# A decoder layer on one core: the input projection's last eight K tiles in two passes for six column blocks, and the modulation's VectorE share as row sums over a transposed copy

## The chip, the core and the metric

One NeuronCore of a Trainium2 chip runs the whole program, with TensorE (PE), VectorE (DVE), ScalarE (ACT), GpSimd (POOL) and SyncE (SP, which here only issues DMAs). The metric is the device time in microseconds (us) of one execution; the time of a kernel is the median of its runs.

## What is computed

A decoder layer for 256 tokens, width 2048, fp32, cut to what matters here:

```python
mod = silu(c) @ w_ada + b_ada                       # w_ada: 2048 x 12288, one vector c
shift_a, scale_a, gate_a, shift_f, scale_f, gate_f = split(mod, 6)
h = rms_norm(x, g_attn_pre) * (1 + scale_a) + shift_a
proj = h @ w_in                                     # 2048 x 5456
# columns: diff q | k | v (1024 each), dsa q (1024) | k | v (128 each), indexer q (1024) | k | w
diff_out = rms_norm((softmax(q1 k1) - lam * softmax(q2 k2)) v)      # 8 heads, causal
score = sum_h w_h * relu(iq_h . ik)                 # 16 indexer heads; the 64 best keys of a query
dsa_out = softmax(q k over those keys) v            # 8 heads
x = x + gate_a * rms_norm([diff_out, dsa_out] @ w_o)
h = rms_norm(x, g_ffn_pre) * (1 + scale_f) + shift_f
x = x + gate_f * rms_norm((silu(h @ w_gate) * (h @ w_up)) @ w_down)
```

## The kernel before

**Weights.** `wload` brings 1 MB of a weight matrix (mostly 4 K tiles of 128 rows by 512 columns) into one of five `raw` buffers. ACT rounds it to `whi` (line 168), DVE subtracts to get the rest `wlo` (line 169), in two halves of 128x1024; there are three buffers of each. A product of a K tile with a token tile is three matmuls (`mm3`, lines 178, 181, 182): 24 matmuls for a megabyte. All these loads stand in the one queue of SP, in the order in which the program issues them.

**Modulation.** The product of silu(c) with `w_ada` is cut into 96 units of 1 MB. `ada_block` makes a unit on PE (line 225: four matmuls, which the trace records as eight) or on DVE (line 233: four `scalar_tensor_tensor` that add a column block times one element of silu(c) to the accumulator `aacc`). 64 units go to PE and 32 to DVE: two of four blocks of the attention gate `Ga`, one of four of `modF` (shift and scale ahead of the FFN), and all of the FFN's gate `Gf`. `ada_step` uses the next unit and keeps two units of loads ahead.

**Projection.** The K tiles are taken in groups of 1, 1, 2, 4 and 8 (`GROUPS`), each a pass over the 11 blocks of 512 columns; after the first pass DVE adds each bank to `PR` (line 733). During a pass the modulation of the next group's rows is made. The last pass, K tiles 8 to 15, goes through the blocks in the order 0, 2, 4, 10, 9, 8, 1, 3, 5, 6, 7. As a block becomes complete, `attend` rotates it and queues jobs: heads of the differential attention (`diff_head`), the indexer's scores (`idx_pairs`, line 422), `top_k` (lines 454 and 455), and the indexed heads (`dsa_pair`). `attn_step` moves every job in flight by one stage, once after each megabyte.

**Output projection and after.** `mixT` holds the attention's output, transposed; K tiles 0 to 7 are the differential heads, 8 to 15 the indexed ones. The first two column blocks of w_o take the rest of the attention along; the other two are made by `tail_pair`, after which `residual` runs for each token tile: the block times the gate into `y` (line 768), the square sum `sst`, its root `rs`, the new `x` (line 843), then the diagonal `dg` (line 848) with which PE makes the transposed `h2` (line 830). The first FFN blocks use only K tiles 0 to 7 of `h2`, while the rest of `modF` is made. Then gate, up and down projections in three groups.

**Order.** The program is scheduled at build time: every engine gets a fixed order of instructions, and an engine waits where its next one is not ready.

## Time and profile before

| | |
|---|---|
| runs | 1273.87, 1273.33, 1276.59 us, median 1273.87 |
| profiled execution, span from first to last instruction | 1272.5 us |
| PE busy | 1233.9 us (97%) |
| DVE busy | 774.3 us (61%) |
| ACT busy | 560.9 us (44%) |
| HBM read | 307.05 MB, 243 GB/s over the span |

The profiled execution's span is 1.4 us under the median time of the runs. Shares of busy time are means over stages that differ: the stages' own bounds are read from tables by window.

### The profile page before, as it was taken

Reading aid. Unit: us, or ns where it says so; the run is one execution under the profiler, and the core shown is the slowest. Engines: PE = TensorE matmul, PEld = TensorE weight load, DVE = VectorE, ACT = ScalarE, POOL = GpSimd, SP = SyncE. Lnnn points to the kernel's source line nnn. Section 1 sums busy time; section 2 is a strip of 40 time slices with the busy share of each in tenths; the row PEclk is TensorE's granted clock in tenths of the full one; section 3 lists DMA queues with packets and bytes.
Section 4 is the critical chain, followed back from the end, with each engine's and each line's share of the span. In section 5 each row is a group of like instructions: output and inputs, shape, how many; then the busy total and the mean of one; then the engine's idle time right before and its main releaser. Section 6 shows DMA issues by size and latency. Waiting matters only on the chain.

```text
span 1272.5 us, 15272 instructions
## 1 busy us (share of the span) xinstructions
PE 1233.9 (97%) x5938; PEld 950.3 (75%) x5938; DVE 774.3 (61%) x1160; ACT 560.9 (44%) x806; POOL 21.4 (2%) x55
## 2 busy tenths in 40 slices
PE   4999999999999999899999999999999999999996
PEld 3666666777666786688887888888888888888885
DVE  3576455898598683758867545754455454445565
ACT  4733333345345543764444444444444334444442
POOL 1000000000000000200000000000000000000000
PEclk8999999999999999999999999999999999999998
DMA  9999997978687487858878656766556555565541
GB/s 307 339 343 327 347 381 278 314 263 321 211 285 268 142 329 289 306 167 286 282 264 290 200 193 222 251 227 198 176 189 199 190 188 190 194 198 182 184 164 66
DMA packets 160090, 310.13 MB, mean 244 GB/s; under 512 B 5785, under 2 KB 19978, under 8 KB 158738
## 3 DMA queue, kind: packets, MB, share of 16 engines
q1 hardware_dynamic: 159938, 309.14, 70.7%
q8 instruction: 46, 0.75, 0.2%
q14 instruction: 26, 0.21, 0.0%
q10 hardware_dynamic: 80, 0.02, 0.0%
HBM read 307.05 MB, written 2.10 MB: 243 GB/s over the span
## 4 chain that ended last, share of the span: by engine, by line
PE 88%; DMA 4%; DVE 4%; issue 1%; ACT 1%; SPq 1%; POOL 0%; DVEq 0%; POOLq 0%; ACTq 0%
PE mm L181 26%; PE mm L178 26%; PE mm L182 25%; PE ad L225 5%; DMA raw<-in_w_ada_dram 4%; DVE aacc L233 2%; DVE wlo L169 1%; PE tr L474 1%; PE tr L411 1%; PE tr L918 1%; PE tr L830 1%; SPq L211 1%; PE tr L392 1%; PE tr L301 0%; PE tr L282 0%
## 5 line engine op out<-in xcount | busy, mean ns | idle before, releaser
L169 DVE TENSOR_TENSOR wlo<-raw,whi 128x1024 fp32r<-128x1024 f32 (+1 forms) x383 | 462.3, 1212 | 338.6 <-ACT whi L168 337.7
L168 ACT ACTIVATE whi<-raw 128x1024 fp32r<-128x1024 f32 (+1 forms) x383 | 400.3, 1050 | 522.4 <-PE mm L182 458.1
L181 PE MATMUL mm<-wlo,h 128*128 128x512 f32 (+1 forms) x1056 | 416.8, 395 | 1.9 <-DVE wlo L169 1.9
L182 PE MATMUL mm<-whi,h 128*128 128x512 f32 (+1 forms) x1056 | 409.9, 389 | 0.2 <-DVE h L335 0.2
L178 PE MATMUL mm<-whi,h 128*128 128x512 f32 (+1 forms) x1056 | 381.4, 394 | 2.4 <-ACT h L330 1.4
L181 PEld LDWEIGHTS mm<-wlo,h 128*128 128x128 f32 x1056 | 198.9, 188 | 62.5 <-issue 9.5
L178 PEld LDWEIGHTS mm<-whi,h 128*128 128x128 f32 x1056 | 196.8, 188 | 63.2 <-issue 13.6
L182 PEld LDWEIGHTS mm<-whi,h 128*128 128x128 f32 x1056 | 198.3, 188 | 42.5 <-issue 3.0
L181 PE MATMUL mm<-wlo,gT 128*128 128x512 f32 x348 | 135.8, 390 | 0.0
L182 PE MATMUL mm<-whi,gT 128*128 128x512 f32 x348 | 135.4, 389 | 0.0
L178 PE MATMUL mm<-whi,gT 128*128 128x512 f32 x348 | 123.0, 390 | 0.0
L233 DVE SCALAR_TENSOR_TENSOR aacc<-raw,csil,aacc 128x512 f32<-128x512 f32 x126 | 94.1, 746 | 23.8 <-DMA raw<-in_w_ada_dram 22.5
L225 PE MATMUL ad<-raw,c 128*32 128x512 f32 (+2 forms) x640 | 79.6, 537 | 9.9 <-DMA raw<-in_w_ada_dram 9.9
L733 DVE TENSOR_TENSOR PR<-mm,PR 128x512 f32<-128x512 f32 (+1 forms) x88 | 57.1, 669 | 41.2 <-PE mm L182 41.0
L182 PEld LDWEIGHTS mm<-whi,gT 128*128 128x128 f32 x348 | 65.3, 188 | 13.8 <-issue 0.2
L181 PEld LDWEIGHTS mm<-wlo,gT 128*128 128x128 f32 x348 | 65.3, 188 | 13.7 <-issue 0.2
L178 PEld LDWEIGHTS mm<-whi,gT 128*128 128x128 f32 x348 | 65.3, 188 | 13.4
L181 PE MATMUL mm<-wlo,mixT 128*128 128x512 f32 x124 | 49.1, 397 | 0.0
L178 PE MATMUL mm<-whi,mixT 128*128 128x512 f32 x124 | 47.5, 400 | 0.6 <-ACT mixT L587 0.6
L182 PE MATMUL mm<-whi,mixT 128*128 128x512 f32 x124 | 46.4, 399 | 0.0
L225 PEld LDWEIGHTS ad<-raw,c 128*32 128x32 f32 x640 | 17.6, 116 | 36.4 <-issue 31.3
L181 PEld LDWEIGHTS mm<-wlo,mixT 128*128 128x128 f32 x124 | 23.3, 188 | 7.8 <-issue 2.5
(195 smaller groups left out, 678.8 us busy)
## 6 DMA issues: line engine op xcount, KB each, us to landing
raw<-in_w_ada_dram SPq DMA_DIRECT2D x96, 1024.0 KB, 7.1
raw<-in_w_gate_dram SPq DMA_DIRECT2D x44, 1024.0 KB, 5.2
raw<-in_w_up_dram SPq DMA_DIRECT2D x44, 1024.0 KB, 5.1
raw<-in_w_down_dram SPq DMA_DIRECT2D x44, 1024.0 KB, 5.2
raw<-in_w_in_dram SPq DMA_DIRECT2D x39, 1024.0 KB, 6.9
raw<-in_w_o_dram SPq DMA_DIRECT2D x16, 1024.0 KB, 5.0
xx<-in_x_dram SPq DMA_DIRECT2D x2, 1024.0 KB
x<-in_x_dram SPq DMA_DIRECT2D x2, 1024.0 KB, 4.7
```

The source lines that it names most:

```text
L168: ACT.activation(hv, src, AF.Copy)
L169: DVE.tensor_tensor(lv, src, hv.bitcast(F32), op=ALU.subtract)
L178: i = PE.matmul(ps, lhsT=hi, rhs=whi, start=start, stop=False)
L181: PE.matmul(ps, lhsT=hi, rhs=wlo, start=False, stop=False)
L182: PE.matmul(ps, lhsT=lo, rhs=whi, start=False, stop=stop)
L211: SP.dma_start(st[b, u], ada_w[u * kk * P:(u + 1) * kk * P, col0s[b]:col0s[b] + n] .rearrange("(k p) n -> p k n", p=P))
L225: PE.matmul(st["ps"][32 * j:32 * j + 32, :n], lhsT=c33[:, k, 1 - b:33 - b], rhs=w, start=(b == 0 and k < 4), stop=(b == nb - 1 and k >= 12 ...
L233: DVE.scalar_tensor_tensor(acc, w, csil[:, k:k + 1], acc, op0=ALU.mult, op1=ALU.add)
L392: PE.transpose(tr[:, i * P:(i + 1) * P], PR[:, t, c0:c0 + P], ident)
L411: PE.matmul(sc[i][:, SEG[t]], lhsT=st["q"][r, (2 * j + t) * P:(2 * j + t + 1) * P], rhs=ikT[r, :P * (t + 1)], start=True, stop=True)
L474: PE.matmul(sc[i][:, SEG[t]], lhsT=l, rhs=r, start=False, stop=(t == T - 1))
L733: DVE.tensor_tensor(dst, banks[c0][t][:, :n], dst, op=ALU.add)
```

## The change

The last group of eight K tiles becomes two groups of four. The six column blocks that come first (`EARLY`) get a pass over K tiles 8 to 11 and one over 12 to 15; the other five (`LATE`) get one pass over all eight, with one more `attn_step` inside each block. The attention's jobs and the loads of `Ga` start with the second of these passes; before that, only A, the modulation that the projection itself needs, is loaded. A unit on DVE is no longer a megabyte of rows of `w_ada`, but 128 rows of a transposed copy `w_adaT` that the host prepares: one `tensor_tensor_reduce` over 128x2048 multiplies it by `csrow` (silu(c) on every partition) and sums along the row, starting from the bias; the result is a column. `spread` turns a column into a row on all partitions: a DVE multiply with the identity, a matmul with ones, and for `csrow` a copy by ACT. On DVE are now the last 4 K tiles of A (8 units), two blocks of `Ga` (8), two of `modF` (16) and all of `Gf` (16): 48 units, and 48 on PE. The two halves of the big shared buffer (`bigB`) are now tiles of their own, `big0` and `big1`.

```diff
-GROUPS = (1, 1, 2, 4, 8)
+GROUPS = (1, 1, 2, 4, 4, 4)
+A_DVE = (5,)
-F_DVE = (2,)
-A_DVE = ()
+F_DVE = (1, 2)
-ATT = 1
+EARLY = (0, 2, 4, 10, 9, 8)
+LATE = (1, 3, 5, 6, 7)
...
+    def ada_rows(col0, dst, bias, finish=None):
...
+        def load():
+            st["raw"] = wp.tile([P, 2048], F32, tag="raw", name=nm("raw"), bufs=RAW)
+            SP.dma_start(st["raw"], w_adaT[col0:col0 + P])
+
+        def use():
+            DVE.tensor_tensor_reduce(out=st["raw"], in0=st["raw"], in1=csrow, scale=1.0, scalar=bias(),
+                                     op0=ALU.mult, op1=ALU.add, accum_out=dst())
+            if finish is not None:
+                after.append(finish)
+
+        units.append((load, use))
+
+    def spread(row, col):
...
+        m = wp.tile([P, 512], F32, tag="aacc", name=nm("dg"), bufs=2)
+        DVE.tensor_tensor(m.rearrange("p (k q) -> p k q", k=4),
+                          ident[:, None, :].to_broadcast([P, 4, P]),
+                          col[:, :, None].to_broadcast([P, 4, P]), op=ALU.mult)
+        ps = tr_bank()
+        PE.matmul(ps, lhsT=ones, rhs=m, start=True, stop=True)
+        if row is None:
+            return ps
+        ACT.activation(row, ps, AF.Copy)
...
+        for i in range(4):
+            ada_rows(c0 + i * P, lambda i=i: part(i),
+                     lambda i=i: bcol[:, col // P + i:col // P + i + 1],
+                     (lambda: DVE.tensor_tensor(g, spread(None, st["g"]), g, op=ALU.mult))
+                     if i == 3 else None)
...
+    passes = [(0, 1, every), (1, 1, every), (2, 2, every), (4, 4, every), (8, 4, EARLY),
+              (12, 4, EARLY), (8, 8, LATE)]
+    for pi, (k0, nk, blks) in enumerate(passes):
+        first, last = pi == 0, pi >= 5
+        if pi == 5:
+            mixT[0] = Halves("mixT", KT)
...
+                        mm3(banks[c0][t][:, :n], *Hs[k], t, whi, wlo, k == k0, k == k0 + nk - 1)
+                    if nk == 8 and k == k0 + 5:
+                        attn_step()
...
-        gT = big.tile([P, 2, 16, S], F32R, tag="bigB", name=nm("gT"))
+        gT = Halves("gT", 16)
```

What this does to the order is shown at three places. First, the queue of SP in the pass over K tiles 4 to 7 (`raw` from `in_w_in` is a weight load, from `in_w_ada` a unit of modulation). Before:

```order
L152 DMA raw_1049<-in_w_in_dram 128x4x512
L211 DMA raw_1091<-in_w_ada_dram 128x4x512
L211 DMA raw_1097<-in_w_ada_dram 128x4x512
L152 DMA raw_1099<-in_w_in_dram 128x4x512
L211 DMA raw_1141<-in_w_ada_dram 128x4x512
L211 DMA raw_1147<-in_w_ada_dram 128x4x512
```

Of the change:

```order
L163 DMA raw_1067<-in_w_in_dram 128x4x512
L220 DMA raw_1109<-in_w_ada_dram 128x4x512
L163 DMA raw_1111<-in_w_in_dram 128x4x512
L220 DMA raw_1153<-in_w_ada_dram 128x4x512
L163 DMA raw_1155<-in_w_in_dram 128x4x512
```

Two units of modulation stood behind each weight load; now one does. From the pass's first weight load to its last the queue held 16 units, and now holds 8.

Second, DVE around the top-k (MAX and MATCH_REPLACE on `nsel`; `mx`, `rcp`, `w`, `s`, `on` and the L641 write of `mixT` belong to the differential heads). Before, in the last blocks of the projection:

```order
L454 MAX m_2456<-nsel 128x8
L484 TENSOR_REDUCE mx_2911<-tr_2902 128x1 x2
L454 MAX m_2456<-nsel 128x8
L455 MATCH_REPLACE nsel<-m_2456,nsel 128x128
L484 TENSOR_REDUCE mx_2911<-tr_2903 128x1 x2
L485 TENSOR_SCALAR mx_2911<-mx_2911 128x2
L455 MATCH_REPLACE nsel<-m_2456,nsel 128x256
L169 TENSOR_TENSOR wlo_3242<-raw_3239,whi_3241 128x1024
L454 MAX m_2456<-nsel 128x8
L485 TENSOR_SCALAR mx_2911<-mx_2911 128x2
L169 TENSOR_TENSOR wlo_3246<-raw_3239,whi_3245 128x1024
```

Of the change, in the first half of the output projection, the last split before the top-k and the first one after it:

```order
L180 TENSOR_TENSOR wlo_3585<-raw_3582,whi_3584 128x1024
L475 SCALAR_TENSOR_TENSOR score<-rl_2611,iwS,score 128x128
L475 SCALAR_TENSOR_TENSOR score<-rl_2611,iwS,score 128x256
L475 SCALAR_TENSOR_TENSOR score<-rl_2650,iwS,score 128x128
L475 SCALAR_TENSOR_TENSOR score<-rl_2650,iwS,score 128x256
L258 ISA raw_3741,modF<-raw_3741,csrow,cols_244 128x2048
```

```order
L614 SCALAR_TENSOR_TENSOR s_3070<-s_3070,w_3145 128x256
L155 TENSOR_SCALAR rs_3138<-ss_3134 128x2
L633 TENSOR_SCALAR on_3133<-tr_3129,rcp_3050,rsd_3137 128x128 x2
L180 TENSOR_TENSOR wlo_3589<-raw_3582,whi_3588 128x1024
L180 TENSOR_TENSOR wlo_3651<-raw_3648,whi_3650 128x1024
```

The weight splits that stood among the rounds of the top-k are gone from there: 90 rows of DVE lie between the splits of the two halves of one `raw`, among them 14 of the 30 rows that add indexer scores (L475), the whole top-k, two of the row sums (L258) and most rows of four differential heads.

Third, DVE at the residual of token tile 0. Before:

```order
L768 TENSOR_TENSOR y<-mm_3920,Ga 128x512
L768 TENSOR_TENSOR y<-mm_3922,Ga 128x512
L839 TENSOR_REDUCE sst<-ssy 128x1
L144 TENSOR_SCALAR rs_4228<-sst 128x1
L843 SCALAR_TENSOR_TENSOR x_3897<-y,ry,x_3897 128x1024 x2
```

Of the change:

```order
L829 TENSOR_TENSOR y<-mm_3844,Ga 128x512
L258 ISA raw_4344,modF<-raw_4344,csrow,cols_244 128x2048
L258 ISA modF 128x1
L829 TENSOR_TENSOR y<-mm_3846,Ga 128x512
L899 TENSOR_REDUCE sst<-ssy 128x1
L258 ISA raw_4347,modF<-raw_4347,csrow,cols_244 128x2048
L258 ISA modF 128x1
L155 TENSOR_SCALAR rs_4122<-sst 128x1
```

Two row sums (each a row over 128x2048 and one that writes the 128x1 result) now stand between `y` and `rs`.

## Rows read from the trace of the kernel before

**Rows 1.** The page: busy time by engine, granted TensorE clock in 40 slices.
```profile
PE 1233.9 (97%) x5938; PEld 950.3 (75%) x5938; DVE 774.3 (61%) x1160; ACT 560.9 (44%) x806; POOL 21.4 (2%) x55
...
PEclk8999999999999999999999999999999999999998
```
**Rows 2.** The page: the chain of work that ended last, by engine.
```profile
PE 88%; DMA 4%; DVE 4%; issue 1%; ACT 1%; SPq 1%; POOL 0%; DVEq 0%; POOLq 0%; ACTq 0%
```
**Rows 3.** Windows by stage: us, busy time and instructions by engine, PEclk, DMA, GB/s.
```profile
112.80:194.50 81.70, 80.94 (x405) 52.25 (x402) 41.83 (x56) 29.62 (x40) 0.00 (x0) 1.00 0.98 358
194.50:283.20 88.70, 88.70 (x430) 61.48 (x429) 67.05 (x140) 35.34 (x66) 1.75 (x3) 1.00 0.80 277
283.20:375.70 92.50, 92.50 (x481) 60.41 (x480) 69.94 (x190) 38.79 (x74) 3.01 (x3) 1.00 0.76 269
375.70:459.00 83.30, 78.27 (x430) 60.31 (x429) 62.15 (x151) 44.67 (x119) 3.86 (x4) 1.00 0.65 228
459.00:518.40 59.40, 57.25 (x274) 40.85 (x272) 36.23 (x44) 24.16 (x35) 4.51 (x6) 1.00 0.84 302
518.40:572.90 54.50, 52.95 (x268) 42.46 (x267) 33.00 (x66) 37.91 (x74) 2.67 (x6) 1.00 0.69 242
708.90:1272.50 563.60, 553.26 (x2469) 457.75 (x2467) 294.89 (x284) 235.94 (x252) 1.11 (x2) 0.99 0.57 189
```
**Rows 4.** Waits from 112.8 to 194.5: us in total, times, longest.
```profile
DVE PR L733 <- PE mm L182: 28.3, 10, 5.3
ACT whi L168 <- DMA raw<-in_w_in_dram: 20.0, 4, 8.3
```
**Rows 5.** A window in the FFN, PE alone: us, busy (x matmuls).
```profile
720.00:795.00 75.00, 75.00 (x330) 1.00 0.62 202
```
**Rows 6.** The chain in order of time, one unit of modulation: start, us.
```profile
111.86 0.99 PE ad L225 x8
```
**Rows 7.** PE on tiles `tr` alone, output projection's first half: us, busy (x).
```profile
375.70:459.00 83.30, 32.50 (x213) 1.00 0.65 228
```
**Rows 8.** DVE groups by form: busy us, mean ns; idle before.
```profile
L169 DVE TENSOR_TENSOR wlo<-raw,whi 128x1024 fp32r<-128x1024 f32 x374 | 455.4, 1223 | 334.9 <-ACT whi L168 334.0
L233 DVE SCALAR_TENSOR_TENSOR aacc<-raw,csil,aacc 128x512 f32<-128x512 f32 x126 | 94.1, 746 | 23.8 <-DMA raw<-in_w_ada_dram 22.5
L733 DVE TENSOR_TENSOR PR<-mm,PR 128x512 f32<-128x512 f32 x80 | 53.5, 686 | 41.2 <-PE mm L182 41.0
...
L961 DVE SCALAR_TENSOR_TENSOR ff<-ff,ry,x 128x512 f32<-128x512 f32 x8 | 5.5, 744 | 0.7 <-POOL ry L145 0.7
...
L843 DVE SCALAR_TENSOR_TENSOR x<-y,ry,x 128x1024 f32<-128x1024 f32 x4 | 5.0, 1281 | 1.8 <-POOL ry L145 1.8
```
**Rows 9.** ACT groups by form: the read of a row sum from the accumulator.
```profile
L487 ACT ACTIVATION_READ_ACCUMULATOR s<-tr,mx 128x1 f32 x48 | 9.7, 203 | 0.0
```
**Rows 10.** DVE by time at the top-k: start, us.
```profile
356.67 0.61 DVE L454 MAX8 m<-score 128x8 f32<-128x128 f32 x2
...
363.43 1.21 DVE L169 TENSOR_TENSOR wlo<-raw,whi 128x1024 fp32r<-128x1024 f32 x1
...
364.82 1.22 DVE L169 TENSOR_TENSOR wlo<-raw,whi 128x1024 fp32r<-128x1024 f32 x1
```
**Rows 11.** All engines by time at the residual: start, us.
```profile
507.03 0.69 DVE L768 TENSOR_TENSOR y<-mm,Ga 128x512 f32<-128x512 f32 x1 [4.45 <-ACT tr L767]
...
508.64 2.48 DVE L843 SCALAR_TENSOR_TENSOR x<-y,ry,x 128x1024 f32<-128x1024 f32 x2 [0.66 <-POOL ry L145]
...
511.64 2.78 PE L225 MATMUL ad<-raw,c 128*32 128x512 f32 x24
...
515.90 0.61 POOL L848 TENSOR_SCALAR dg<-ident,r 128x128 f32<-128x128 f32 x1
```
**Rows 12.** DMA issues: count, KB each, median us from issue to landing.
```profile
raw<-in_w_ada_dram SPq DMA_DIRECT2D x96, 1024.0 KB, 7.1
...
x<-in_x_dram SPq DMA_DIRECT2D x2, 1024.0 KB, 4.7
```

More of the change, by code (lines that the diff above doesn't have):

```diff
@@ L276, in ada_cols, with finish @@
         m, k0 = n // P, col // P
-        def finish(accs):
+        d = dst[:, :, k0:k0 + m]
+        def finish(acc):
             ps = tr_bank()
             for i in range(m):
-                if len(accs) == 1:
-                    PE.matmul(ps[:, 2 * i:2 * i + 2], lhsT=accs[0][:, i * P:(i + 1) * P], rhs=sel,
-                              start=True, stop=True)
-                else:
-                    for b in range(2):
-                        PE.matmul(ps[:, 2 * i + b:2 * i + b + 1], lhsT=accs[b][:, i * P:(i + 1) * P],
-                                  rhs=ones[:, 0:1], start=True, stop=True)
-            d = dst[:, :, k0:k0 + m]
-            DVE.tensor_tensor(d, ps[:, :2 * m].rearrange("p (m b) -> p b m", b=2),
-                              bcol.rearrange("p (b k) -> p b k", b=2)[:, :, k0:k0 + m], op=ALU.add)
-            DVE.scalar_tensor_tensor(d[:, 1], d[:, 1], 1.0, g[:, k0:k0 + m], op0=ALU.add, op1=ALU.mult)
@@ new lines, in finish, with gain @@
+            DVE.tensor_tensor(d, ps[:, :2 * m].rearrange("p (m b) -> p b m", b=2),
+                              bcol().rearrange("p (b k) -> p b k", b=2)[:, :, k0:k0 + m], op=ALU.add)
+            gain()
+        def gain():
+            DVE.scalar_tensor_tensor(d[:, 1], d[:, 1], 1.0, g()[:, k0:k0 + m], op0=ALU.add, op1=ALU.mult)
+        if on_pe:
+            ada_block([chunk * D + col, (chunk + 1) * D + col], n, finish)
+            return
+        for k in range(k0, k0 + m):
+            for b in range(2):
+                ada_rows((chunk + b) * D + k * P, lambda b=b, k=k: dst[:, b, k:k + 1],
+                         lambda b=b, k=k: bcol()[:, 16 * b + k:16 * b + k + 1],
+                         gain if (k, b) == (k0 + m - 1, 1) else None)
@@ new lines, in ada_gate, with finish, part @@
+    def ada_gate(G, chunk, col, on_pe, bcol):
+        c0 = chunk * D + col
+        g = G[:, col:col + 512]
+        if on_pe:
+            def finish(acc):
+                ps = tr_bank()
+                PE.matmul(ps, lhsT=ones, rhs=acc, start=True, stop=True)
+                DVE.tensor_tensor(g, ps, g, op=ALU.mult)
+            ada_block([c0], 512, finish, b_ada[0:1, c0:c0 + 512])
+            return
+        st = {}
+        def part(i):
+            if i == 0:
+                st["g"] = const.tile([P, 4], F32, tag="gcol", name=nm("gcol"), bufs=2)
+            return st["g"][:, i:i + 1]
+        for i in range(4):
[3 more added lines that the diff above has]
+                     if i == 3 else None)
@@ L643, in layer @@
     late_rows()
-    cols2 = to_cols(R2, 49, "cols2")
-    gF, bF = cols2[:, 0:16], cols2[:, 16:48]
+    cols2 = to_cols(R2, 81, "cols2")
+    gF, bF, bGa, bGf = cols2[:, 0:16], cols2[:, 16:48], cols2[:, 49:65], cols2[:, 65:81]
+    csrow = ct([P, D], "csrow")
+    for a in range(0, KT, 4):
+        spread(csrow[:, a * P:(a + 4) * P], csil[:, a:a + 4])
     g08 = ct([P, 1], "g08")
@@ L689, in layer @@
     need_f2 = len(units)
-    k0 = 0
-    for gi, nk in enumerate(sizes):
-        first, last = gi == 0, gi == len(sizes) - 1
-        if last:
-            mixT[0] = big.tile([P, 2, KT, S], F32R, tag="bigB", name="mixT")
+    every = tuple(range(11))
+    passes = [(0, 1, every), (1, 1, every), (2, 2, every), (4, 4, every), (8, 4, EARLY),
[4 more added lines that the diff above has]
+            mixT[0] = Halves("mixT", KT)
             tc.keep_in_program_order(SP.dma_start(Ga, g_attn_post[0].partition_broadcast(P)))
-        if gi == 2:
+        if pi == 2:
             lamv = wp.tile([P, 4, 64], F32, tag="hf", name="lamv", bufs=2)
@@ L708, in layer @@
         W = {1: 2048, 2: 1024}.get(nk, 512)
-        spans = [(c, min(W, NPROJ - c)) for c in range(0, NPROJ, W)]
-        if last:
-            spans = [(512 * ci, min(512, NPROJ - 512 * ci)) for ci in order]
+        if W > 512:
+            spans = [(c, min(W, NPROJ - c)) for c in range(0, NPROJ, W)]
+        else:
+            spans = [(512 * ci, min(512, NPROJ - 512 * ci)) for ci in blks]
         blocks = [(si, a) for si in range(len(spans)) for a in range(k0, k0 + nk, 4)]
@@ L737, in layer @@
                 ada_step(RATE[bi % len(RATE)])
-                for _ in range(ATT):
-                    attn_step()
+                attn_step()
                 jobs.extend(newjobs)
@@ L790, in side @@
         ada_step(1)
-        for _ in range(ATT):
-            attn_step()
+        attn_step()
     def need_mix(ks):
@@ L974 @@
 def kernel(**inputs):
+    inputs["w_adaT"] = np.asarray(inputs["w_ada"])[0].T
     arrays = {n: np.ascontiguousarray(inputs[n]) for n in NAMES}
```

116 lines of the change are left out of this document (54 added, 62 removed).

## The prediction

> **What bounds the kernel now.** I read the page's busy shares first. PE has work for 1233.9 of 1272.5 us, DVE for 61% and ACT for 44%, and the granted clock is below its upper level only in the first slices and the last [rows 1]. The chain that ended last agrees: 88% of it is PE, 4% DMA, 4% DVE [rows 2]. So the change can win in two ways: less work for PE, or the 38.6 us in which PE is idle. It can lose by making another engine late. A mean over 1272 us cannot say which, so I cut the span at the stages' first and last matmuls.
>
> In the pass over K tiles 4 to 7 the DMA queues are busy 0.98 of the time at 358 GB/s, while DVE waits 28.3 us for PE's banks and ACT 20.0 us for weights [rows 3, 4]. That pass runs into memory and PE at once. In the blocks after it (194.5 to 375.7, first the six early ones, then the five late ones) PE is busy throughout, DMA only 0.76 to 0.80, and DVE 67.05 of 88.7 and 69.94 of 92.5 us. In the output projection's first half PE is busy 78.27 of 83.3 us, DVE 62.15. From 708.9 on the FFN runs on PE alone with DVE at 295 of 564 us [rows 3]. So slack on DVE is plenty after 709 and thin (about 20 us a stage) between 194 and 459, where the change adds to DVE.
>
> **Unit prices.** A matmul of 128x512 takes 75.00/330 = 0.227 us in a steady stretch [rows 5]. A megabyte of weights is 24 of them, 5.45 us. A unit of modulation on PE costs 0.99 us in the chain [rows 6]. On DVE a unit was four instructions of 746 ns, 2.98 us. A row sum appears nowhere in this trace. Two rows bound it. The cheapest form over the same megabyte is the subtraction, two at 1223 ns: 2.45 us. Of instructions with two fp32 sources in SBUF, 512 columns take 744 ns and 1024 take 1281, that is 1.049 ns a column, so 2048 would take 744 + 1536 x 1.049 = 2355 ns [rows 8]. Its result needs a read of the accumulator, of which only ACT's form has a row, 203 ns [rows 9]. I take 2355 + 150 = 2.5 us, and as the upper end the old form's 2.98.
>
> The Trainium skill ("Vector Engine (DVE) Microarchitecture Reference", section 7, "Points that are easy to get wrong") says that a scalar_tensor_tensor with two SBUF sources that are not bf16 halves throughput, since no port is left for reading the accumulator back. The rows show such an instruction at 1281 ns for 1024 columns, which is no slower than the slope between sizes asks, but without an accumulator. By the rule a sum over 2048 columns would take about twice my price, and the total would be that of the rival below named half rate, 1310 us.
>
> **The change, part by part.**
>
> *Pass over K tiles 4 to 7.* The queue loses 8 of its 16 units (11 weight loads and 8 units are 19.9 MB, which at 358 GB/s is 56 us), so memory no longer decides. PE keeps 264 matmuls, 59.9 us. In the instruction order 20 modulation matmuls remain in this stage (5 units, 5 us), and the small products behind them are 2 us. That is 67 us, plus 1 for what fails to overlap: **68 against 81.7, -13.7**. The modulation that left is not gone. Eight units come back in the next pass, on DVE.
>
> *Early blocks in two passes.* The matmuls are the same 288, 65.4 us. There are 12 more additions into `PR` at 686 ns [rows 8], 8 us of DVE that PE does not wait for as long as four banks rotate. The first pass (K tiles 8 to 11) has 6 weight loads and 8 units or a little more: some 14.7 MB, 41 us at 358 GB/s, against 35 us of PE work. Memory decides there. Its DVE work is 36 us with the sums (6 to 8 of them at 2.5), so DVE is close behind. The second pass has 32.7 us of matmuls, 23 modulation matmuls (6 us) and the first transposes (3 us): 42 us. Together **83 against 88.7, -5.7**.
>
> *Late blocks.* 240 matmuls are 54.5 us; 15 modulation matmuls and some 53 of attention bring PE to 67. Before, PE was full for 92.5 us here [rows 3], for much more of the attention was made in this stretch. DVE: I summed the rows of the new order at the trace's durations and scaled by 0.87, since rows overlap at their ends (in the output projection's first half 71 us of rows made 62.15 busy). This gives 68 us. Two engines at 67 and 68 that feed one another do not overlap fully; I take 74, **-18.5**.
>
> *Output projection's first half.* Here the work lands that left the stretch before. PE: 192 matmuls (43.6 us), 5 units, and 226 other instructions in place of 145. At the trace's 32.50/213 = 0.153 us each [rows 7], the 81 more are 12 us, so PE's 78.27 us become 91 to 95. DVE's rows sum to 110, 95 after scaling. Both are longer than the old stage, and they do not run side by side. The top-k used to stand in the late blocks with weight splits in between (MAX8 from 356.67, splits at 363.43 and 364.82 [rows 10]). Now 90 rows of DVE lie between two splits, 42 us by their rows and 36 scaled. PE meets in the same place 54 rows without one weight matmul, 8 to 10 us of work, and its next weight matmuls need a differential head that comes after the top-k on DVE: 27 us of DVE rows. PE is therefore idle for some 12 to 17 us. I add 12 to PE's 94, and 2 for the short waits that the stage has today: **108 against 83.3, +24.7**. From both sides: 95 when nothing waits (DVE's sum alone), 128 when the whole block of 36 us stands still.
>
> *Rest.* The second half of w_o loses 5 units on PE (5 us), but two sums stand between the `y` and `rs` of token tile 0. Today this chain ends with `y` at 507.03, `x` at 508.64 and the last `dg` at 515.90, and PE has only 2.78 us of modulation to put into its wait [rows 11]. Two sums are 5 us later: net 0. The first FFN blocks take 14 units in place of 7, that is 7.3 MB on top of 242 GB/s x 54.5 us = 13.2; at 358 GB/s 57.3, with 1.2 for what does not overlap 58.5 against 54.5, +4. `Gf` has 16 sums (40 us) in place of 64 instructions (48 us) under a PE that alone sets the time: 0. `csrow` (four multiplies, matmuls and copies, 1 us each) lies in stages that wait for DMA: 0, or +1 where that cover is gone. Rows of 8 KB from `w_adaT` in place of rows of 2 KB: a megabyte of `x` in such rows lands in 4.7 us, one of `w_ada` in 7.1 [rows 12], under less load; I take no difference, or a gain within the 41 us of the first early pass. Together **+4**, 0 to +9 (the upper end has the residual's 5 us unhidden).
>
> **Sum.** -13.7 - 5.7 - 18.5 + 24.7 + 4 = -9.2. The profiled span of 1272.5 becomes 1263.3; the runs' median stands 1.4 above that span, so 1264.7 us.
>
> **The rivals.** I count as no change what stays within 0.3% (1270.1 to 1277.7), about what a measurement of this kernel can tell.
>
> *The backlog hides.* Jobs move from the late blocks into w_o, and both engines stay full: late blocks and first half then take DVE's 68 + 95 plus the 5 us that PE is idle there today, 168 instead of my 182. All that the lighter passes win is kept. For it: PE's order and DVE's are planned together, and before the two stages lost only 5 us. Against it: the 90 rows without a split. 1263.3 - 14 + 1.4 = 1251, or 1245 if the early passes also meet PE's 77 us.
>
> *DVE becomes the bound in w_o's first half* (the other side). Each head's softmax waits for the top-k's rounds on DVE, PE waits for the head, and w_o's matmuls start only behind all that: PE's 48 us of other work and the 36 us of DVE in a row, then 43.6 us of matmuls, 128. That is +20 on my sum; with the residual's sums not hidden by anything (+5) 1290. It is slower than before from 120 us in this stage on (1276). For it: DVE gains some 33 us in a stage with 21 to spare. Against it: w_o's matmuls on ready splits, three buffers deep, cover 8 us.
>
> *Sums at half rate.* As an accumulator costs a second read or pass, a sum takes 2 x 2355 + 150 = 4.9 us. Some 24 of the 48 sums lie in the late blocks, w_o and the residual, where DVE sets the pace: 24 x 2.4 = 58 us, of which some 45 show: 1310.
>
> *Little moves.* PE's saved units come back as waits, and memory's total of 307 MB is unchanged: 1270 to 1277.
>
> **How the numbers follow.** My forecast 0.43 (own range 1254 to 1275: faster 0.33, same 0.09, slower 0.01); backlog hidden 0.17 (1244 to 1252, faster); DVE the bound 0.26 (1278 to 1298, slower); half rate 0.06 (1300 to 1320, slower); little moves 0.08 (same). So faster 0.50, same 0.17, slower 0.33. The price of a sum at 2.98 adds 0.5 x 24 = 12 us at most and stays inside. The range runs from 1246 to 1294: it leaves out 0.06 of the half rate, the far end of the DVE case and the lowest of the second case, less than 0.2.
>
> **What would show it.** Right: the pass over K tiles 4 to 7 in 66 to 70 us with DMA under 0.9; row sums of 2.4 to 2.6 us; a hole in PE of 10 us or more in w_o's first half, that ends behind `on` or `mixT` of a head, with MAX8 and MATCH_REPLACE busy on DVE; `rs` of token tile 0 later against the last w_o matmul by about 5 us. Wrong: sums near 4.9 us; the early passes over 86 us together (then DVE or the loads held the banks); w_o's first half under 97 or over 125 us; or the gain of the first pass lost in the next one, where the eight units on DVE hold back the splits.

## The result, and the profile after

The changed kernel takes 1320.24 us (median of four runs, 1317.19 to 1320.39), the kernel before 1274.51 beside it: a ratio of 1.0352, 95% interval 1.0336 to 1.0368. The forecast of 1264.7 and its range, 1246 to 1294, are missed: a gain was forecast, and the kernel became slower. The profiled execution has a span of 1318.3 us, 45.8 more than before.

The page of the changed kernel: busy time by engine, then the granted clock and the memory rate in 40 slices of 33 us (compare [rows 1]).

```profile
PE 1243.0 (94%) x5786; PEld 956.5 (73%) x5786; DVE 810.2 (61%) x1147; ACT 565.8 (43%) x808; POOL 19.9 (2%) x49
...
PEclk8999999999996999799999999999999999999998
...
GB/s 311 274 356 299 272 346 355 242 347 353 242 233 2 162 269 308 260 279 230 307 256 282 231 174 198 276 242 173 187 189 193 191 192 192 193 190 190 192 160 64
```

PE has 16 units of modulation less to do and is yet busy for 9 us more, and in one slice memory moves 2 GB/s. The windows by stage show where (the columns are those of [rows 3]; in order: K tiles 0 to 3, pass over 4 to 7, first and second early pass, late pass, w_o's first half, second half, the FFN's first blocks and the rest of them).

```profile
29.00:119.50 90.50, 89.00 (x443) 55.52 (x440) 57.82 (x88) 44.03 (x68) 0.00 (x0) 0.99 0.85 307
119.50:188.30 68.80, 68.80 (x315) 50.22 (x314) 47.73 (x56) 26.54 (x31) 0.00 (x0) 1.00 0.85 307
188.30:228.60 40.30, 36.19 (x161) 27.68 (x161) 32.42 (x40) 15.55 (x20) 0.00 (x0) 0.96 1.01 368
228.60:274.90 46.30, 46.30 (x212) 29.66 (x211) 31.30 (x65) 15.07 (x19) 0.00 (x0) 1.00 0.76 269
274.90:345.70 70.80, 70.80 (x339) 51.73 (x338) 61.93 (x134) 31.94 (x64) 3.91 (x2) 1.00 0.82 297
345.70:486.00 140.30, 116.02 (x574) 80.31 (x574) 97.28 (x248) 60.64 (x161) 4.14 (x6) 0.91 0.51 178
486.00:544.80 58.80, 49.29 (x217) 39.35 (x216) 46.37 (x49) 24.20 (x35) 5.64 (x6) 0.92 0.90 323
544.80:609.10 64.30, 61.79 (x298) 43.01 (x298) 26.50 (x43) 32.64 (x55) 1.66 (x4) 0.97 0.74 260
609.10:660.40 51.30, 47.23 (x212) 37.39 (x211) 41.45 (x58) 27.81 (x44) 0.00 (x0) 1.00 0.72 250
```

By these boundaries (the same numbers of matmuls in both kernels), against before:

| stage | before | forecast | after | after - before |
|---|---|---|---|---|
| K tiles 0 to 3 | 83.8 | 83.8 | 90.5 | +6.7 |
| K tiles 4 to 7 | 81.7 | 68 | 68.8 | -12.9 |
| early blocks, K tiles 8 to 15 | 88.7 | 83 | 86.6 | -2.1 |
| late blocks | 92.5 | 74 | 70.8 | -21.7 |
| w_o, first half | 83.3 | 108 | 140.3 | +57.0 |
| w_o, second half | 59.4 | 59.4 | 58.8 | -0.6 |
| FFN's first blocks, both parts | 98.9 | 102.9 | 115.6 | +16.7 |
| from there to the end | 655.2 | 655.2 | 657.9 | +2.7 |

From K tile 4 to the last projection matmul all that was forecast came, 226.2 us against 225. The loss lies behind it. Where it stands still is seen in windows of 10 us:

```profile
390.00:400.00 10.00, 3.47 (x22) 2.17 (x23) 10.00 (x46) 2.31 (x9) 0.00 (x0) 0.78 0.32 105
400.00:410.00 10.00, 8.04 (x28) 4.64 (x25) 7.85 (x34) 4.45 (x18) 0.69 (x1) 0.50 0.01 2
410.00:420.00 10.00, 9.74 (x39) 7.05 (x38) 3.95 (x14) 3.41 (x13) 0.69 (x1) 0.70 0.00 0
420.00:430.00 10.00, 7.97 (x43) 5.95 (x43) 6.77 (x16) 6.80 (x22) 0.69 (x1) 1.00 0.11 22
```

From 390 on DVE is full and PE nearly empty (3.47 of 10 us); then PE's clock is at 0.50, that is 1.2 GHz, and memory moves nothing for 20 us. The waits of SP (line and what it waited for, us in total, times, longest) and two rows of its timeline:

```profile
SPq L255 <- DVE wlo L180: 109.7, 28, 36.2
```

```profile
391.18 0.37 SPq L163 DMA_DIRECT2D raw<-in_w_o_dram  x1
427.88 0.34 SPq L255 DMA_DIRECT2D raw<-in_w_adaT_dram  x1
```

For 36.7 us no load is issued. SP waits for a buffer whose split stands on DVE behind the top-k and four heads. DVE by time (start, us), the pair of splits on either side of the block and, between them, the top-k's end:

```profile
377.08 2.35 DVE L180 TENSOR_TENSOR wlo<-raw,whi 128x1024 fp32r<-128x1024 f32 x2
...
404.82 0.36 DVE L512 TENSOR_SCALAR nselb<-nsel 128x384 bf16<-128x384 f32 x1
...
426.63 2.36 DVE L180 TENSOR_TENSOR wlo<-raw,whi 128x1024 fp32r<-128x1024 f32 x2 [0.72 <-ACT whi L179]
```

This is the block of 90 rows. It took 47 us; the estimate was 36. Windows over the block and over what is left of the stage behind it (columns as above):

```profile
379.40:426.60 47.20, 33.81 (x136) 21.21 (x133) 35.04 (x124) 17.88 (x61) 2.07 (x3) 0.75 0.23 79
426.60:486.00 59.40, 48.52 (x265) 39.47 (x266) 39.35 (x78) 27.49 (x70) 0.69 (x1) 1.00 0.55 191
```

In the block DVE is busy for 35.0 us, which is the estimate, and waits for the other 12.2. PE is idle for 13.4 us in it, and for 10.9 more behind it.

### The profile page after: what moved, and what is told of

Its sections match the earlier page's. It is cut to its first block, busy times and chain, and to the rows that moved or that the text cites. A ratio compares the mean times of both kernels' runs of the same rounds, so it can differ in the third digit from the quotient of the medians.

```text
span 1318.3 us, 14947 instructions
## 1 busy us (share of the span) xinstructions
PE 1243.0 (94%) x5786; PEld 956.5 (73%) x5786; DVE 810.2 (61%) x1147; ACT 565.8 (43%) x808; POOL 19.9 (2%) x49
## 4 chain that ended last, share of the span: by engine, by line
PE 78%; DMA 8%; DVE 8%; issue 3%; ACT 2%; SPq 1%; POOL 0%; DVEq 0%; POOLq 0%; ACTq 0%
PE mm L192 23%; PE mm L189 23%; PE mm L193 23%; DMA raw<-in_w_adaT_dram 6%; PE ad L231 4%; DVE wlo L180 3%; DVE raw L258 2%; DMA raw<-in_w_ada_dram 1%; PE tr L527 1%; PE tr L978 1%; DMA rows<-in_b_ada_dram 1%; PE tr L890 1%; PE tr L272 1%; SPq L220 1%; ACT whi L179 1%
## 5 line engine op out<-in xcount | busy, mean ns | idle before, releaser
L180 DVE TENSOR_TENSOR wlo<-raw,whi 128x1024 fp32r<-128x1024 f32 x383 | 461.6, 1212 | 348.5 <-ACT whi L179 348.1
L179 ACT ACTIVATE whi<-raw 128x1024 fp32r<-128x1024 f32 x383 | 401.0, 1051 | 529.9 <-PE mm L193 477.8
L258 DVE CUSTOM_DVE_ANT_0 raw<-raw,csrow,cols 128x2048 f32<-128x2048 f32 x48 | 112.6, 2346 | 40.6 <-DMA raw<-in_w_adaT_dram 40.6
L231 PE MATMUL ad<-raw,c 128*32 128x512 f32 (+2 forms) x512 | 72.4, 532 | 19.8 <-DMA raw<-in_w_ada_dram 19.7
L796 DVE TENSOR_TENSOR PR<-mm,PR 128x512 f32<-128x512 f32 (+1 forms) x100 | 64.5, 667 | 20.4 <-PE mm L193 20.0
L192 PEld LDWEIGHTS mm<-wlo,gT 128*128 128x128 f32 x348 | 65.3, 188 | 13.6 <-issue 0.2
L189 PEld LDWEIGHTS mm<-whi,mixT 128*128 128x128 f32 x124 | 23.7, 191 | 11.3 <-ACT mixT L586 4.6
```

Source lines behind the costliest of these rows:

```text
L179: ACT.activation(hv, src, AF.Copy)
L180: DVE.tensor_tensor(lv, src, hv.bitcast(F32), op=ALU.subtract)
L189: i = PE.matmul(ps, lhsT=hi, rhs=whi, start=start, stop=False)
L192: PE.matmul(ps, lhsT=hi, rhs=wlo, start=False, stop=False)
L231: PE.matmul(st["ps"][32 * j:32 * j + 32, :n], lhsT=c33[:, k, 1 - b:33 - b], rhs=w, start=(b == 0 and k < 4), stop=(b == nb - 1 and k >= 12 ...
L258: DVE.tensor_tensor_reduce(out=st["raw"], in0=st["raw"], in1=csrow, scale=1.0, scalar=bias(), op0=ALU.mult, op1=ALU.add, accum_out=dst())
```

## The experiments

The change's parts were undone one at a time or done alone, and jobs were moved. The table gives, for all kernels, the time, the late pass and w_o's first half together, then for this half alone its length, PE's idle time and granted clock (from a window over it, as above), and both parts of the FFN's first blocks. One execution each, except for the change and the two that have an interval in their text. (The change's own four runs lie 3.2 us apart.) Beside them the kernel before took 1274.0 to 1274.6.

| kernel | us | late + w_o | w_o half | PE idle | PEclk | FFN first |
|---|---|---|---|---|---|---|
| before | 1274.5 | 175.8 | 83.3 | 5.0 | 1.00 | 98.9 |
| changed | 1320.2 | 211.1 | 140.3 | 24.3 | 0.91 | 115.6 |
| modF on PE | 1312.9 | 202.8 | 132.0 | 13.2 | 0.94 | 120.9 |
| one pass | 1304.0 | 210.0 | 118.7 | 21.7 | 0.86 | 97.0 |
| passes only | 1309.6 | 194.8 | 96.0 | 4.4 | 1.00 | 123.8 |
| more steps | 1312.3 | 206.8 | 126.8 | 24.9 | 0.89 | 118.2 |
| indexer first | 1315.1 | 206.6 | 122.8 | 24.4 | 0.90 | 115.6 |
| rate 2 | 1309.7 | 219.2 | 118.4 | 23.9 | 0.88 | 98.3 |
| one pass, PE | 1308.4 | 190.5 | 86.8 | 2.2 | 1.00 | 99.3 |
| short top-k | 1311.1 | 204.9 | 134.1 | 19.8 | 0.92 | 115.6 |
| form only | 1302.9 | 202.8 | 105.5 | 10.8 | 0.94 | 98.7 |
| two passes, PE | 1320.8 | 206.7 | 102.6 | 6.9 | 1.00 | 122.1 |
| passes, rate 2 | 1308.5 | 213.9 | 101.8 | 12.1 | 0.93 | 96.7 |
| block first | 1288.8 | (other passes) | 74.7 | 2.8 | 1.00 | 96.7 |
| old form | 1308.1 | 194.6 | 99.2 | 13.0 | 0.93 | 124.8 |
| csrow late | 1315.0 | 212.2 | 143.0 | 24.8 | 0.89 | 115.7 |
| one modF block | 1306.6 | 198.5 | 127.7 | 12.5 | 0.97 | 115.9 |

**Modulation of modF on PE.**

```diff
-F_DVE = (1, 2)
+F_DVE = ()
```

> The changed kernel (1320 us) with all of modF's modulation back on PE (F_DVE empty): 16 of 48 row sums gone, those that stand on DVE in the output projection and at the residual; PE gets 16 units of 1 us. Theory A, late attention (the two passes complete the six early blocks' columns later, so the top-k and most heads fall into w_o, where 91 rows of DVE without a weight split stop the ring of five raw buffers): the stop stays, 87 rows in the order here, and w_o's first half stays at 125 to 140 us, the whole at 1305 to 1325. Theory B, row sums in the ring (DVE waits in order for a sum's load that is queued behind weight loads, 40.6 us in all): w_o's first half falls from 140 to about 110, the whole to 1280 to 1295.

Measured 1312.9, w_o's first half 132.0. Fewer sums, half of the idle time, but 16 units more on PE; A's range, with the queue's stop shortened (longest wait of SP 20.3 us, 36.2 in the change).

**One pass.**

```diff
-    passes = [..., (8, 4, EARLY), (12, 4, EARLY), (8, 8, LATE)]
+    passes = [..., (8, 8, EARLY), (8, 8, LATE)]
```

> The changed kernel with one pass over K tiles 8 to 15 for the six early blocks, as before the change; row sums, the late pass and its additional attention step are kept. Theory A: the first head starts some 30 us earlier against the last projection matmul, w_o's first half falls from 140 to 85 to 105 us, the whole to 1270 to 1290. Theory B: the sums in w_o are still there, the whole stays at 1305 to 1320. Third theory, C: whatever the passes, it is the block of DVE rows without a split that costs; the order here still has 85 rows in one block, so it would stay over 1300 for this reason as well, with a stop of 30 us or more in the DMA queue.

Measured 1304.0, idle 21.7. The stop is there without the passes (SP's longest wait is 27.1 us, a little under C's 30), so theory A alone falls.

```profile
373.60:492.30 118.70, 97.01 (x457) 71.34 (x456) 89.03 (x223) 50.97 (x136) 2.75 (x4) 0.86 0.53 182
```

**Passes only**, on the kernel before, with `GROUPS`, `EARLY`, `LATE` and the loop of the change.

> The kernel before (1274 us) with the change's passes and additional attention step alone: the modulation is cut, placed and computed as before, no row sums. Theory A: the attention is as late as in the change, w_o's first half over 115 us, the whole 1295 to 1320. Theory B: no sums in the ring, 1255 to 1275. Theory C: the longest block of DVE rows without a split has 46 rows (half of the change's 91), so a stop of about half the length: 1275 to 1295.

Measured 1309.6, for another reason: w_o's first half has idle 4.4, so no stop (theory A's 115 us are missed, C's stop too). Against before the late pass and this half are 19 us longer, the FFN's first blocks 25 (windows over both parts, then the page's busy time by engine):

```profile
528.80:602.30 73.50, 70.34 (x322) 45.22 (x322) 33.57 (x54) 32.91 (x55) 3.57 (x6) 0.98 0.76 262
602.30:652.60 50.30, 48.01 (x212) 38.55 (x211) 42.80 (x67) 27.79 (x44) 0.00 (x0) 0.97 0.72 248
...
PE 1254.5 (96%) x5938; PEld 956.8 (73%) x5938; DVE 781.0 (60%) x1172; ACT 563.9 (43%) x806; POOL 21.8 (2%) x55
```

These are the same 5938 PE instructions as before the change [rows 1], and in this order they keep PE busy for 20.6 us more and leave it idle for 14.7 more. Of the 20.6 us, 13.3 are in the modulation's records; why they take longer in other places is not shown.

**More steps.** The first heads here read the columns of block 4 before their second pass is added, so the values differ; the work is the same.

```diff
-                    if nk == 8 and k == k0 + 5:
+                    if nk == 8 and k in (k0 + 1, k0 + 3, k0 + 5) or pi == 5 and k == k0 + 1:
```

> The changed kernel with more attention steps: three in place of one inside each late block, and one more in each block of the second early pass, so that the jobs are issued earlier in the program. Theory A: earlier issue brings the attention forward by 10 to 30 us, the whole 1285 to 1310. Theories B and C: the order still has 82 rows in a block and all sums, so no change, 1310 to 1325.

Measured 1312.3, between the two. The attention starts 14 us sooner and its last head is 8 us sooner.

**Indexer first.**

```diff
-EARLY = (0, 2, 4, 10, 9, 8)
+EARLY = (10, 9, 8, 0, 2, 4)
```

> The changed kernel with the early blocks in the order 10, 9, 8, 0, 2, 4: the indexer's columns first, so that the top-k runs in the late pass among weight splits (splits 81 to 89 of 96 in DVE's order, where the change has none left). Everything else stays: two passes, all row sums. Theory A', cover: the time of the change is lost because the last matmul with weights on hand is spent before the top-k begins; with the top-k moved, the stop of 36 us in the DMA queue falls under 20 us, w_o's first half from 140 to 115 to 125 us, the whole to 1295 to 1305. Theory D, chain: the attention takes 200 to 220 us from its first scores to its last head whatever stands around it, and w_o's first half ends 6 us after it; the first scores come from blocks that are now complete last (some 35 us later), so the end does not move or moves back: 1315 to 1335.

Measured 1315.1, at the edge of D. The top-k ended at 351 in place of 405 us, the last indexed head at 478.1 in place of 481.1. The queue's stop is shorter (longest wait of SP 24.3 us, where A' asked for under 20), but idle stays at 24.4 us: PE's longest waits are for rows of the heads (`s`, `mixT`), as in the change. So a place for the top-k alone is not what lacked.

**Rate 2.**

```diff
-RATE = (1, 1, 1, 2)
+RATE = (2,)
```

> The changed kernel with two units of modulation in each block of the last two passes (RATE 2, in place of 1, 1, 1, 2): the eight units that the change leaves behind for the first FFN blocks are made earlier. If the 17 us that the first FFN blocks lost (115.6 in place of 98.9 for both parts) come from these units, that stretch returns to 96 to 100 us. The attention also comes earlier in the order (indexer from matmul 947 in place of 1066), but the units load the late pass: there +8 to +15 us, and w_o's first half -10 to -25. The whole 1290 to 1305; if the late modulation is not what holds the FFN, 1310 to 1325.

Measured 1309.7. The FFN's first blocks return to 98.3 us, as forecast, but the late pass grows by 30 us, from 70.8 to 100.8, where 8 to 15 were expected, and gives back most of what is won (w_o's first half is 22 us shorter). The whole lies in neither range. The two parts of the FFN's first blocks:

```profile
553.90:607.60 53.70, 52.50 (x250) 43.78 (x250) 31.08 (x64) 35.79 (x73) 1.67 (x4) 0.94 0.45 146
607.60:652.20 44.60, 44.60 (x202) 36.75 (x201) 36.66 (x37) 22.12 (x24) 0.00 (x0) 1.00 0.84 301
```

**One pass, attention's modulation on PE**: the one-pass kernel without the additional step and with `GA_DVE = F_DVE = ()`.

> One pass over K tiles 8 to 15 as before the change, no additional attention step, and no row sums for the attention's gate and modF (those 32 units on PE); sums stay for A's last four K tiles and for the FFN's gate. If the row sums on DVE are what delays the attention with one pass (w_o's first half 118.7 us and 1304 in that run), it goes back to the speed of before: first scores to last head 205 to 220 us, w_o's first half 80 to 95 us, the whole 1272 to 1290 (6 us of the start stay lost). If something else of the change is the cause (the split shared buffer, the late order), 1295 to 1310.

Measured 1308.4, so the whole is missed by 18 us. w_o's first half is as forecast, with no stop. But 24 units (not 32) have gone back to PE. Against the kernel before, 16 more units of the gate and of modF stand on PE (8 more in the whole program, as A has 8 on DVE), and it is full for 206.6 us in the passes over the early and the late blocks in place of 181.2:

```profile
198.90:301.80 102.90, 102.90 (x491) 64.24 (x489) 56.10 (x130) 38.70 (x77) 1.39 (x2) 1.00 0.70 239
301.80:405.50 103.70, 103.70 (x506) 63.43 (x506) 66.71 (x188) 39.70 (x77) 2.13 (x3) 1.00 0.70 241
405.50:492.30 86.80, 84.61 (x477) 58.61 (x476) 43.66 (x108) 42.06 (x106) 2.07 (x3) 1.00 0.73 254
```

**Short top-k**, two rounds of eight.

```diff
-            for r in range(r0, r0 + 2):
+            for r in range(r0, r0 + 2 if r0 == 0 else r0):
```

> The changed kernel with two of the top-k's eight rounds (six rounds, some 11 us of DVE rows, are left out, so the selected keys differ; all else stays, in the same order). If DVE's block of rows between two splits is on the path, the whole falls by 7 to 11 us, to 1309 to 1313, and w_o's first half with it. If the loads behind the block set the time (ring and memory), it falls by less than 4 us, 1316 to 1321.

Measured 1311.1, 9.1 us less for some 11 us of DVE rows, 6.2 of it in w_o's first half: DVE's block is on the path there. (The other 3 us lie behind the FFN's first blocks, which no theory here explains.)

**Form only**: one pass, no additional step, `A_DVE = ()`, `F_DVE = (2,)`.

> The change without its passes and without its shift of work: one pass over K tiles 8 to 15, no additional attention step, the same units on DVE as before the change (two blocks of the attention's gate, one of modF, all of the FFN's gate), only made as row sums over the transposed copy. DVE has 16 x (2.98 - 2.43) = 9 us less in the attention's stages. If a row sum is harmless by itself, first scores to last head stay at 205 to 215 us and the whole at 1272 to 1282 (the start keeps its 6 us, csrow on PE). If the row sum's form is what delays the attention (2.35 us that nothing can pass, in order, behind a load), the stop in w_o's first half appears here too: PE idle over 10 us there, the whole 1288 to 1305.

Measured 1302.9, ratio to before 1.0224 (1.0209 to 1.0239). Row sums in the old places leave PE idle for 10.8 us in w_o's half, just inside the range given for the form. But the change's long stop of the queue is not here: SP's longest wait for a split is 12.5 us, before it was 11.0 (waits of SP here, then before):

```profile
SPq L255 <- DVE wlo L180: 56.4, 17, 12.5
...
SPq L152 <- DVE wlo L169: 642.0, 136, 11.0
```

Of the 22 us by which the half is longer than before, 16.4 are PE's work (94.7 in place of 78.3), as more of the attention falls into it (40.9 us on `tr` in place of 32.5) and more of the units (7.7 in place of 3.0).

**Two passes, attention's modulation on PE**: the changed kernel with `GA_DVE = F_DVE = ()`.

> The changed kernel with the passes kept and none of the attention's gate or modF on DVE: 24 row sums gone, 24 units more on PE; sums stay for A's last four K tiles and the FFN's gate. If the row sums take the cover away (in the order the top-k now stands among the last weight splits again, 91 to 95 of 96), PE's idle time in w_o's first half falls from 24 us to under 8, but PE has 24 us more: the whole 1300 to 1318. If the passes alone bring the stop, idle stays over 18 us and the whole goes to 1325 to 1345.

Measured 1320.8, a little over the first range: idle 6.9, and SP's longest wait for a split 11.5 us, so the stop goes with the sums, passes or not. PE then has the work, and the late pass takes 104.1 us in place of 70.8.

**Passes, rate 2**: the passes-only kernel with `RATE = (2,)`.

> The change's passes alone on the kernel before, as in the run with 1309.6 us, with two units of modulation a block in the last two passes. If the 25 us that its first FFN blocks lost come from units left behind, both parts of these blocks return from 123.8 to 97 to 102 us and the whole to 1285 to 1295; the units stand in the late pass instead, which may cost 5 to 10. If not: 1305 to 1315.

Measured 1308.5. The FFN's first blocks come back to 96.7, as forecast, but the whole doesn't: the late pass and w_o's half lose 19 us more, so the units cost nearly as much in the one place as in the other.

**Block first**, on the kernel before.

```diff
+    passes = [(0, 1, every), (1, 1, every), (2, 2, every), (4, 4, EARLY), (8, 8, EARLY), (4, 12, LATE)]
```

> The kernel before with another order of passes: K tiles 4 to 7 for the six early blocks only, then 8 to 15 for these, then 4 to 15 for the five late blocks; nothing else changed. The early columns are complete some 20 us sooner, and the late blocks have 50 per cent more matmuls to cover the attention. Theory D (the attention needs some 200 to 215 us from first scores to last head, and w_o's first half ends 6 us after it): first scores at 215 to 228, last head at 425 to 440, the whole 1250 to 1264. Theory P (PE's work of 1234 us is the bound wherever the attention stands, and the pass over K tiles 4 to 7 is bound by memory with PE idle 10 us): last head at 445 to 460, the whole 1270 to 1285.

Measured 1288.8, ratio 1.0116 (1.0093 to 1.0138): worse than both theories gave. First scores at 223.1 us, 17.6 sooner than before, last head at 472.7, 20 us later: D, a chain of fixed length, falls. The pass bound by memory leaves PE idle 9.3 of 62.6 us, as P had it:

```profile
112.40:175.00 62.60, 53.33 (x285) 32.96 (x282) 24.16 (x37) 19.25 (x30) 0.00 (x0) 0.95 1.04 382
```

**Old form**: the passes-only kernel with the change's `A_DVE = (5,)` and `F_DVE = (1, 2)`.

> The kernel before with the change's passes and the change's placement of units (the last four K tiles of A, two blocks of the attention's gate, two of modF and the FFN's gate on DVE), each unit made in the old form, four instructions of 746 ns on rows of w_ada; no transposed copy. DVE has 0.55 us more a unit than with row sums. In the order the top-k keeps weight splits beside it (from 90 to 96 of 96, none in the change). If the row sum's form makes the stop, PE's idle time in the attention's stages is under 14 us (28.4 in the change) and the whole 1295 to 1312, in spite of more DVE work; if the placement makes it, idle 24 to 35 and the whole 1318 to 1335.

Measured 1308.1. From the pass over K tiles 4 to 7 to the end of w_o's half PE is idle for 21.7 us (28.4 in the change, 9.7 with the passes only). The time falls in the first range, the idle time in neither, so both take part. In w_o's half alone PE is idle for 4.4 us with the passes only, 13.0 with the change's placement added, and 24.3 with the row sums added to that. SP's longest wait is here 20.9 us, behind the old form's instructions:

```profile
SPq L213 <- DVE aacc L235: 62.4, 19, 20.9
```

In time, the late pass and w_o's half are as long as with the passes only (194.6 and 194.8) and 16.5 us longer in the change; the change gets part of that back in other stages, 9.2 of it in the FFN's first blocks. Of the 12 us to the change, some 7 are the start, where `csrow` is missing here.

**csrow late.**

```diff
+            for a in range(0, KT, 4):
+                spread(csrow[:, a * P:(a + 4) * P], csil[:, a:a + 4])
```

> The changed kernel with the four products that spread silu(c) moved from the start to just before the pass over K tiles 2 and 3. If they cost the start its 6.7 us (PE is nearly full there and they are 4 us of it), the first two passes end 3 to 6 us sooner and the whole is 1313 to 1317, unless the pass that takes them is as full: then no change, 1317 to 1321.

Measured 1315.0, 5.2 us less, and K tiles 0 to 3, which still hold the four products (now in their second pass), take 86.0 in place of 90.5:

```profile
28.60:114.60 86.00, 85.44 (x453) 55.77 (x451) 58.51 (x91) 44.48 (x69) 0.00 (x0) 0.99 0.92 330
```

**One block of modF on DVE.**

```diff
-F_DVE = (1, 2)
+F_DVE = (2,)
```

> The changed kernel with one block of modF on DVE in place of two (as before the change): 16 row sums in the attention's stages in place of 24, 8 units more on PE. By the number of sums, PE's idle time from the pass over K tiles 4 to 7 to the end of w_o's first half lies between the run with 8 (17.1) and the change with 24 (28.4): 20 to 26 us; PE's work is 8 us more, part of it inside idle time; the whole 1312 to 1322.

Measured 1306.6, with PE idle for 16.6 us in that stretch, both below their ranges: the time is 13.6 us less than the change's although PE has 8 units more. So it isn't the number of sums that counts, for with 8 of them PE was idle for 17.1. The eight sums that go are those that stand in and behind the top-k's block (from 368 to 471 us). The other eight, in w_o's second half, gain 6.3 us where they are (1312.9 without them).

## Why the prediction was wrong

**The step that failed** is the one on w_o's first half: "I add 12 to PE's 94, and 2 for the short waits that the stage has today". Measured were 116.0 us of PE work and 24.3 idle. Of the 55 us between the forecast span and the measured one, 32.3 are in this step (140.3 in place of 108) and 21.5 in the term of +4. The place and the kind were right (a hole that ends behind the heads, MAX8 and MATCH_REPLACE on DVE in it), and so was PE's idle time in it. Two terms were not: the 94 us of PE's work, and the 2 us for all other waits.

1. The hole. I took the 27 us of DVE rows up to the first head less 8 to 10 us of PE work. The block's 36 us were durations without a wait. DVE is busy for 35.0 us in it, but it also waits for 12.2, for PE above all, then for ACT and POOL, and 1.1 us for the loads of sums. PE's idle time there came out at 13.4 us all the same, because PE's own work in the block went slower (point 3). The sums' waits for loads lie mostly in other places. Before, DVE waited 22.5 us for modulation's loads in the whole program [rows 8]; the sums wait 40.6:

```profile
L258 DVE CUSTOM_DVE_ANT_0 raw<-raw,csrow,cols 128x2048 f32<-128x2048 f32 x48 | 112.6, 2346 | 40.6 <-DMA raw<-in_w_adaT_dram 40.6
```

2. What follows the hole. I let the stage go on with 2 us of waits; PE is idle for 10.9 us there. The ring was full and SP stood 36.7 us, so the loads of the second part came one by one, each released by DVE (178 GB/s over the half, 228 before [rows 3]). The longest waits of PE from 426.6 to 486.0 name steps of the heads, none a split or a weight load; DVE, which works in its order, has row sums ahead of such steps and waits for their loads:

```profile
DVE raw L258 <- DMA raw<-in_w_adaT_dram: 6.5, 4, 3.1
...
PE mm L189 <- ACT mixT L586: 3.7, 3, 2.2
...
PE mm L193 <- DVE mixT L587: 1.9, 1, 1.9
...
PE tr L548 <- DVE s L572: 1.8, 2, 1.4
```

3. PE's work. Windows over w_o's first half, then over the block and what is behind it, with PE's instructions on `tr` alone, the attention's products above all:

```profile
345.70:486.00 140.30, 63.93 (x341) 0.91 0.51 178
...
379.40:426.60 47.20, 27.75 (x112) 0.75 0.23 79
426.60:486.00 59.40, 20.60 (x144) 1.00 0.55 191
```

I had 294 records at 0.153 us; there were 341 at 0.187. 47 more records are 7 us, the slower rate 12, and the slow records are those of the block (0.248 us each; 0.143 behind it). The rate is PE's clock, at 0.75 over the block: a matmul that takes 0.227 us [rows 5] takes 0.43 in the hole (the chain in order of time: start, us).

```profile
414.30 0.43 PE mm L189
...
448.12 0.68 PE mm L193 x3
```

PE idles, the clock goes to 0.50, and the attention's own matmuls, which are what everything waits for, run at half speed. By windows of 5 us (busy time times one less the clock) this costs 10.4 us from 119 to 486, 9.1 of it in the block, and 4.4 from there to 660, at the residual, against nothing before from 112 to 660.

**The rest, +4, was +25.5.**

- "`csrow` ... lies in stages that wait for DMA: 0, or +1 where that cover is gone": +6.7. PE was busy 81.98 of 83.8 us there before, so it had little room for them (PE by time; four products of two records each, 4.0 us together):

```profile
37.18 1.92 PE L272 MATMUL tr<-dg,ones 128*128 128x512 f32 x4
...
41.68 1.02 PE L272 MATMUL tr<-dg,ones 128*128 128x512 f32 x2
...
43.22 1.02 PE L272 MATMUL tr<-dg,ones 128*128 128x512 f32 x2
```

  Moving them gave 5.2 back, although they stayed within K tiles 0 to 3. So most of the 6.7 comes of their place at the start; in what way, no run shows.
- The FFN's first blocks: +16.7 where I had +4. I priced the 7 additional loads by memory alone. They are also 5 units of PE work, and the second half of `h2` waits for them: PE is busy for 109.0 us there and idle for 6.6, before for 97.4 and 1.6 ([rows 3] and, for the second part before the change, this window):

```profile
572.90:617.30 44.40, 44.40 (x201) 36.85 (x200) 38.99 (x47) 21.93 (x24) 0.00 (x0) 1.00 0.86 292
```

  With the units made earlier these blocks are at 98.3 and 96.7 us, so the late units are the cause; but made earlier they cost the attention's stages nearly as much.
- The residual: two sums before `rs`, as said (DVE by time). From w_o's last matmul (530.68) to the first FFN one (544.84) 14.2 us pass, 7.1 before; PE's longest wait in it, 7.2 us, ends with the load of a unit. The half's net of 0 held.

```profile
528.48 2.34 DVE L258 CUSTOM_DVE_ANT_0 raw<-raw,csrow,cols 128x2048 f32<-128x2048 f32 x1
...
530.75 0.15 DVE L155 TENSOR_SCALAR rs<-sst 128x1 f32<-128x1 f32 x1
```

**Right** were the price of a sum (2.5 us forecast, 2346 ns and a read of 80) and the pass over K tiles 4 to 7 (68 and 68.8). In two more the number came by a somewhat different way, which is luck in part. The first early pass (41 and 40.3) was bound by memory as forecast, but only four of its eight sums stand in it; the other four ran in the pass before. In the late pass (74 and 70.8) PE was full for all of it and DVE busy for 61.9, where I had two engines at 67 and 68 that don't quite overlap. The likeliest rival on the other side, "DVE becomes the bound in w_o's first half", comes nearest to what happened: 145 of the half's 193 matmul records with weights start only at 414 us or later, behind the top-k and the first head after it. But DVE is busy for just 97.3 of the 140.3 us, so the order on DVE holds the stage rather than the sum of DVE's work. That rival was given 0.26 and 128 us for the stage, and even that was short of 140.3.

**What was gained was moved.** Before the change PE was idle 5.8 us in the whole stretch from 112.8 to 459. By busy time no more than these 5.8 us could be won there by filling gaps; the rest had to be work taken off PE. The change took 16 units off, and the passes put off attention into a place with no weights to multiply beside it. Most of the 24 us that the early and late blocks gained are that attention: PE's work on `tr` there fell from 38.7 to 15.5 us, and in w_o's first half it rose from 32.5 [rows 7] to 63.9 and came back dearer. Most of the 13 us of the pass over K tiles 4 to 7 are units that went to DVE or later (PE's work on units there: 17.7 us before, 8.4 after). With the sums of the gate and of modF gone the stop goes (idle 2.2 and 6.9 us), but then PE has the units: 1308 and 1321 us. And the passes alone, with no stop and no row sum, take 1309.6 us, so the stop is how the change loses its time, and not the only way to lose it. No kernel here beats the one before.

**Open.** Every edit also gives a new order on every engine. In the form-only kernel the indexer's products begin at 321.5 us, before at 299.9, and whether that is the sum's own time, or where the plan put other work, is not separated; a kernel with the old order and another form was not tried. Block first's late pass of 138.8 us is PE's work, full from end to end: by tiles, 92.7 us on weights, 35.8 on `tr` and 21.8 on units, where the late blocks had 62.5, 24.3 and 13.2 before. Why its last head comes 20 us later although its first scores come sooner is not shown.

## What to carry to other kernels

When a stage gets shorter because work leaves it, find where that work goes and what runs beside it there: with PE at 98% in a stretch there is little to win but work removed. An in-order queue that loads for two consumers stops for both when one of them stands behind a long block, as SP's did here; search the order for the longest run without a buffer release, and price it with its waits (47 us here), not with busy time (35). The idle TensorE cost twice here, once as the hole and once as a lower clock on the very products that end it. Count as well what waits behind the block: 13.4 us of PE's idle time lie in it and 10.9 after it.

## What the hardware showed

A multiply with a sum along the row, over 128x2048 with both sources fp32 in SBUF, took 2346 ns, and the read of its result 80 ns. That is close to what the form without a sum gives for 2048 columns, 2355 ns (744 ns for 512 and 1.049 ns for each column more [rows 8]). The Trainium skill ("Vector Engine (DVE) Microarchitecture Reference", section 7, "Points that are easy to get wrong") says that the scalar_tensor_tensor form loses half its throughput with two such sources; it did not hold for this instruction, and for scalar_tensor_tensor itself no run here has an accumulator.

A megabyte in rows of 8 KB landed in 6.6 us, in rows of 2 KB in 7.6 within the same kernel (medians from issue to landing):

```profile
raw<-in_w_ada_dram SPq DMA_DIRECT2D x48, 1024.0 KB, 7.6
raw<-in_w_adaT_dram SPq DMA_DIRECT2D x48, 1024.0 KB, 6.6
```

The two kinds stand in different stages, so the length of the rows is not shown to be the reason. The first early pass ran at 368 GB/s, but only two of the 14 loads issued in it are of the former kind.
